# Gate projections as seven block products, with the pre-activations kept in memory

## The chip, the cores and the metric

The kernel runs on one core of one Trainium2 chip. It is one program with one launch. The metric is the time of one execution on the device in microseconds. Three runs of the kernel before took 1441.94, 1443.87 and 1445.47 us; the median is 1443.87 us.

A core has a matrix engine (PE, with its weight loads listed as PEld), a vector engine (DVE), a scalar engine (ACT), a general engine (POOL) and a queue that starts most of the transfers (SP). They run beside each other and wait for each other by semaphores.

## The reference

One layer of a decoder is applied to 1024 prompt tokens and to 64 sample tokens with the same weights. Cut to what the change touches:

```python
p = rms_norm(x, ln1) @ w_in                 # [a | q | k | v | g_a | g_b]
a, q, k, v, g_a, g_b = split(p)             # g_a, g_b: 1024 columns each
a_mix = pooling(a)                          # 512 columns
attn  = dilated_attention(q, k, v)          # 256 columns
mixed = sigmoid(g_a) * (a_mix @ w_pa) + sigmoid(g_b) * (attn @ w_pb)
h = x + mixed @ w_o
y = h + relu(rms_norm(h, ln2) @ w_up)**2 @ w_down
```

All is float32. The widths are: model 1024, pooling 512, attention output 256, feed-forward 4096. The key and value caches of the sample group are also given back, shifted by 8 positions.

## The kernel before, in words

**Layout.** Activations lie transposed: channels on the 128 partitions, tokens along the free axis. All 1088 tokens (`TOK`) are held together, in an order that puts tokens with the same remainder modulo 4 side by side. Two tiles, `act_t[0]` and `act_t[1]`, hold the normalized input as a high and a low part in the narrower float32r form (`split`, lines 113 to 116: ACT writes the high part, DVE subtracts it from the source for the low part). A product of two numbers is made of three passes, high by high, high by low and low by high (`PASSES`). A float32 product of a 128-channel block by a 128-channel block is therefore three PE instructions.

**Weights.** Weights arrive in panels of 256 output columns. `fetch` starts the load of 512 columns into one of three `raw` tiles, and `split` writes the high and low parts into `places`, a tile with room for three panels. `panel` does so at once; `line_up` and `feed` do it ahead of need, paced by PE. `behind_pe` adds a wait of an instruction on a given matrix product, by default the last one that had been issued when the line ran.

**Order.** PE's order is the order of the program text. On the other engines a planner orders the instructions ahead of time, and each engine and each queue then runs its own list in order.

**Stages.** First the pooling input, then q, k and v for the three head groups with the attention blocks between them. Attention's blocks are generators: `step` moves every active one by a yield, and the gate products call it twice per unit, so that the last attention blocks run among the first gate products.

**The gates and the branches** (lines 1163 to 1268). `gate` computes one unit: 128 output channels by a chunk of 384 or 320 tokens, 24 PE instructions, then DVE multiplies by the inverse norms `rb_g` (line 1176) and ACT applies the sigmoid (line 1178). Panels `ga0`, `ga1` and the start of `gb0` run while attention ends. When it has ended, `branches` reads pooling and attention results back (`raw_b`) and splits them into `ab`. Then a loop over d = 0 to 3 takes 256 output channels at a time: six units of g_a, six of g_b, and for each unit `pa_` (four channel blocks of w_pa, 12 instructions) and `pb_` (6 instructions with w_pb). DVE multiplies and adds; the result is split. Since `act` is still being read by later gates, the first six of the eight 128-channel blocks of the result are stored to memory (`mix_d`) and come back over POOL's queue (line 1267) at the end; the last two are written directly.

**After that**, w_o runs by token halves of 544 tokens as two times 272 columns (`ph`), and the feed-forward layer forms both its products from seven block products: `products` computes 24 instructions of 128x272 (line 1477), `put` splits a quarter of weights (lines 1403 and 1404), and `run` works a queue of (prepare weights, products, post) with preparation three entries ahead and loads a given number of entries ahead. The copies of the shifted caches (line 1794) are spread over the whole run by waiting on chosen weight splits.

## Time and profile before

| What | Value |
|---|---|
| Median of three runs | 1443.87 us |
| Profiled execution | 1445.38 us |
| Its span, first to last instruction | 1443.6 us |
| PE busy | 1428.8 us (99%) |
| PE weight loads busy | 1376.5 us (95%) |
| DVE busy | 884.7 us (61%) |
| ACT busy | 718.2 us (50%) |
| POOL busy | 230.6 us (16%) |
| Mean granted PE clock | 0.996 |
| Moved by transfers | 279.04 MB, mean 193 GB/s |

The page of the profile starts with the busy time of each engine and its share of the span. It then shows the chain of work that ended last, followed back from the last instruction, as shares by engine and line; the same chain can be listed in order of time. Groups of instructions are listed by line, engine, operation and tile as "out<-in", with the busy time of the group, the mean duration of one in ns, and after the second bar the idle time of the engine just before them with what ended it. A window row gives, for a stretch of time, its length, and the busy time of each engine with the number of instructions in brackets, then the granted PE clock, the share of the transfer engines and the rate moved.

### The profile page before, as it was taken

Reading aid. Unit: us, or ns where it says so; the run is one execution under the profiler, and the core shown is the slowest. Engines: PE = TensorE matmul, PEld = TensorE weight load, DVE = VectorE, ACT = ScalarE, POOL = GpSimd, SP = SyncE. Lnnn points to the kernel's source line nnn. Section 1 sums busy time; section 2 is a strip of 40 time slices with the busy share of each in tenths; the row PEclk is TensorE's granted clock in tenths of the full one; section 3 lists DMA queues with packets and bytes.
Section 4 is the critical chain, followed back from the end, with each engine's and each line's share of the span. In section 5 each row is a group of like instructions: output and inputs, shape, how many; then the busy total and the mean of one; then the engine's idle time right before and its main releaser. Section 6 shows DMA issues by size and latency. Waiting matters only on the chain.

```text
span 1443.6 us, 28367 instructions
## 1 busy us (share of the span) xinstructions
PE 1428.8 (99%) x10765; PEld 1376.5 (95%) x10765; DVE 884.7 (61%) x1685; ACT 718.2 (50%) x1904; POOL 230.6 (16%) x297
## 2 busy tenths in 40 slices
PE   9999999999999999999999999999999999999998
PEld 8988877878899999999999999999999999999998
DVE  7665575766764552425567877656665586664566
ACT  9566755778634222214435545545444444444453
POOL 1711355555500100000000000000000000000100
PEclk9999999999999999999999999999999999999999
DMA  6311788744555654539656667566567987677574
GB/s 212 111 48 61 215 195 219 199 113 99 148 148 161 208 193 156 183 85 284 210 177 219 225 221 247 184 212 225 186 196 243 320 281 252 219 228 228 183 265 173
DMA packets 169303, 279.04 MB, mean 193 GB/s; under 512 B 33735, under 2 KB 88333, under 8 KB 167118
## 3 DMA queue, kind: packets, MB, share of 16 engines
q1 hardware_dynamic: 161390, 226.89, 50.3%
q0 software_dynamic: 7776, 50.34, 11.0%
q8 instruction: 84, 1.38, 0.4%
q14 instruction: 53, 0.43, 0.1%
HBM read 216.56 MB, written 104.26 MB: 222 GB/s over the span
## 4 chain that ended last, share of the span: by engine, by line
PE 94%; DVE 2%; ACT 1%; DMA 1%; issue 1%; POOL 1%; SPq 0%; DVEq 0%; POOLq 0%; ACTq 0%
PE pd L1755 23%; PE pz L1477 22%; PE ph L184 7%; PE pga L184 7%; PE pgb L184 7%; PE pqk L184 6%; PE pv L184 4%; PE pa L184 3%; PE a L306 3%; PE pb L184 2%; PE pq L184 1%; PE pk L184 1%; DMA raw_qkv<-in_w_in_dram 1%; PE sg0b L637 1%; PE pog0b L667 1%
## 5 line engine op out<-in xcount | busy, mean ns | idle before, releaser
L1755 PE MATMUL pd<-places 128*128 128x272 f32 x2688 | 334.7, 287 | 0.0
L1755 PEld LDWEIGHTS pd<-places 128*128 128x128 f32 x2688 | 334.6, 188 | 0.0
L1403 ACT ACTIVATE places<-raw_d 128x544 fp32r<-128x544 f32 (+1 forms) x176 | 110.8, 646 | 159.9 <-DMA raw_d<-z_d 63.1
L1404 DVE TENSOR_TENSOR places<-raw_d,places 128x544 fp32r<-128x544 f32 (+1 forms) x176 | 122.4, 711 | 94.2 <-ACT places L1403 92.8
L1794 POOL DMA_DIRECT2D out_kv_sample_dram<-in_cache_kv_dram x96 | 47.0, 492 | 830.8 <-ACT places L1403 531.3
L1477 PE MATMUL pz<-act,places 128*128 128x272 f32 x912 | 119.2, 289 | 0.0
L1477 PEld LDWEIGHTS pz<-act,places 128*128 128x128 f32 x912 | 116.5, 188 | 0.0
L184 PE MATMUL pga<-act,places 128*128 128x384 f32 (+1 forms) x576 | 100.5, 333 | 0.0
L184 PE MATMUL pgb<-act,places 128*128 128x384 f32 (+1 forms) x576 | 97.9, 327 | 0.0
L184 PEld LDWEIGHTS pga<-act,places 128*128 128x128 f32 x576 | 96.7, 191 | 0.8 <-issue 0.6
L184 PE MATMUL ph<-act,places 128*128 128x272 f32 x768 | 97.3, 289 | 0.0
L184 PEld LDWEIGHTS ph<-act,places 128*128 128x128 f32 x768 | 96.5, 188 | 0.3 <-ACT places L114 0.2
L184 PEld LDWEIGHTS pgb<-act,places 128*128 128x128 f32 x576 | 95.4, 188 | 0.0
L1477 PE MATMUL pz<-act,apart 128*128 128x272 f32 x624 | 82.0, 289 | 0.0
L1477 PEld LDWEIGHTS pz<-act,apart 128*128 128x128 f32 x624 | 79.9, 188 | 0.1
L600 POOL TENSOR_TENSOR mr<-ms,mhalf 128x4 f32<-128x4 f32 (+2 forms) x39 | 52.3, 1342 | 105.1 <-DVE ms L599 105.0
L184 PE MATMUL pqk<-places,act 128*128 128x512 f32 x240 | 61.0, 403 | 1.1 <-ACT qk L605 1.1
L1477 PE MATMUL pz<-places 128*128 128x272 f32 x432 | 56.4, 287 | 0.0
L184 PEld LDWEIGHTS pqk<-places,act 128*128 128x128 f32 x240 | 44.6, 192 | 11.2 <-ACT qk L605 1.3
L1477 PEld LDWEIGHTS pz<-places 128*128 128x128 f32 x432 | 55.0, 188 | 0.0
L805 POOL TENSOR_TENSOR pck<-pck,qs 128x256 f32<-128x256 f32 x64 | 47.9, 780 | 44.0 <-DMA pck<-in_cache_kv_dram 25.5
L184 PE MATMUL pa<-ab,places 128*128 128x384 f32 (+1 forms) x288 | 51.4, 326 | 0.0
(390 smaller groups left out, 2623.7 us busy)
## 6 DMA issues: line engine op xcount, KB each, us to landing
out_kv_sample_dram<-in_cache_kv_dram POOLq DMA_DIRECT2D x72, 480.0 KB, 5.4
raw_d<-z_d SPq DMA_DIRECT2D x112, 272.0 KB
z_d<-t SPq DMA_DIRECT2D x84, 272.0 KB
raw_d<-in_w_down_dram SPq DMA_DIRECT2D x80, 256.0 KB
raw_u<-in_w_up_dram SPq DMA_DIRECT2D x64, 256.0 KB
raw_qkv<-in_w_in_dram SPq DMA_DIRECT2D x36, 256.0 KB
pck<-in_cache_kv_dram SPq DMA_DIRECT2D x32, 256.0 KB
pcv<-in_cache_kv_dram SPq DMA_DIRECT2D x32, 256.0 KB
```

Source lines behind the costliest of these rows:

```text
L184: last_mm[0] = t_.matmul(out, lhs(a, k), rhs(b, k), start=(j == 0), stop=(j == len(terms) - 1))
L306: last_mm[0] = t_.matmul(pts[m][:, :n], wt[:, a, kk, m * P:(m + 1) * P], act4[b][kk][:, :, part4(c)], start=(p == 0 and kk == 0), stop=(p ...
L600: g_.tensor_tensor(r[:n, :H], ms[:n, :H], mhalf[:n, :H], op=ALU.pow)
L637: t_.matmul(sc[e][:, hp, j * P:(j + 1) * P], qT[rows, hp, :], kT[rows, 2 + hp, :], start=True, stop=True)
L667: t_.matmul(po[e * HD:(e + 1) * HD, hp, :], vr[:, h * HD:(h + 1) * HD], pTs[e][:, hp * nk + j, :], start=(j == 0), stop=(j == nk - 1))
L805: behind_pe(g_.tensor_tensor(t[:, n], t[:, n], qs[:, :256], op=ALU.mult))
L1403: ins = s_.activation(view(t[:, 0]), src, AF.Copy)
L1404: v_.tensor_tensor(view(t[:, 1]), src, view(t[:, 0]).bitcast(F32), op=ALU.subtract)
L1477: last_mm[0] = t_.matmul(x[:, c, :Q], A[:, a, k * P:(k + 1) * P], Bv(b, k, c), start=(first and n == 0), stop=(n == len(terms) - 1), skip_ ...
L1755: last_mm[0] = t_.matmul(chain[t][:, c, :Q], A[:, a, t * P:(t + 1) * P], Z[:, b, c * Q:(c + 1) * Q], start=(fresh and f == 0 and n == 0), ...
L1794: ins = g_.dma_start(d, a)
```

## The change

Both gate projections take the form that the feed-forward layer already has. Each panel of 256 gate columns is a product of a 2 by 2 block matrix of weights (output halves m, input halves a) with a 2 by 2 block matrix of the input (input halves, token halves j of 544 tokens). It is formed from seven block products instead of eight, using sums of weight blocks and sums of input blocks.

- In the early phase, while attention ends, the two products "11" and "21" of each of the eight panels run (16 products of 24 instructions, two banks each). They use the first token half. The first is written to memory (`pg_d`), the accumulated pair is one quarter of the result (`g_d`). `step` is called after each half product and once more after the product.
- `make_sums(k)`, called after products 3, 5, 7 and 9, reads the rows of x for one channel block of each input half (tile `gx`, one buffer), scales them by ln1 and the inverse norms, and forms the sums T1, T3, T2, the block "22" and T4. T1 and "22" overwrite the second token half in `act`; T2 and T3 go to `places`; T4 goes through memory (`t4_d`).
- `finish_attention` closes the attention pools and changes the PSUM layout; it is tried after every fourth product.
- The other five products of each panel (`gate_group`) go through the queue of `enqueue` and `run`, with `load_gate` bringing the panel. The results are pre-activations and are stored to `g_d`.
- The second linear products with w_pa and w_pb run by token halves: all four weight panels stay in `places` (`put_ab`), `ab_part` reads back pooling and attention results, `ab_unit` reads two rows of `g_d`, applies the sigmoids, multiplies, adds and splits straight into `act`. `mix_d` is no longer used.
- The cache copies wait on the weight splits of the gate stage (`marks_g`) instead of `throttle`. Several helpers (`right`, `products`, `put`, `run`) move up in the text; `step` of the feed-forward queue is renamed `enqueue`, and `later` there `lazy`.

```diff
+    def make_sums(k):
+        v = [gx.tile([P, H], F32, name=f"gv{n}_{k}", tag=f"gv{n}") for n in range(4)]
+        for a in range(2):
+            x = gx.tile([P, TOK], F32, name=f"gx{a}_{k}", tag="gx")
+            kk = 4 * a + k
+            dma(x, i["xT"][:, kk, :])
+            for j in range(2):
+                v_.scalar_tensor_tensor(two(v[2 * a + j]), by_token(x, j), ln1[:, kk:kk + 1], two(rb_g[:, half(j)]),
+                                        op0=ALU.mult, op1=ALU.mult)
+        v11, v12, v21, v22 = v
+        def sum_to(n, out, a, b):
+            v_.tensor_tensor(out, a, b, op=ALU.subtract)
+            split(*(t[:, k, :] for t in T[n]), out)
+        sum_to(1, v11, v12, v11)
+        sum_to(3, v12, v22, v12)
+        sum_to(2, v11, v22, v11)
+        split(*(t[:, k, :] for t in T["22"]), v22)
+        v_.tensor_tensor(v21, v21, v11, op=ALU.subtract)
+        dma_st(t4_d[k], v21)
...
+    for n, (f, a) in enumerate(order):
+        fetch_first(n + 5)
+        if a == 0:
+            open_x[f] = bank_pair(f"pg{f}")
+        products(open_x[f], ready.pop(n), B["21" if a else "11"], a == 0, between=step)
+        ready[n + 3] = put_first(n + 3)
+        t = row_tile(1 + a, f)
+        for c in range(2):
+            v_.tensor_tensor(two(t)[:, c], open_x[f][c][:, :Q], rb_g[:, c * Q:(c + 1) * Q], op=ALU.mult)
+        dma_st(g_d[f, 0][:, half(0)] if a else pg_d[f], t)
+        if n in (3, 5, 7, 9):
+            make_sums((n - 3) // 2)
+        step()
+        if n % 4 == 3 and psx is None and not active and not waiting:
+            finish_attention()
...
+    for k in range(4):
+        t = row_tile(2, f"t4_{k}")
+        dma(t, t4_d[k])
+        split(T[4][0][:, k, :], T[4][1][:, k, :], t)
...
+    def load_gate(f):
+        raws[f] = [rr(gq, [P, 1024], F32, name=f"rawg{f}_{a}", tag="rawg", bufs=4) for a in range(2)]
+        for n in range(0, 2048, 512):
+            behind_pe(dma(raws[f][n // 1024][:, n % 1024:n % 1024 + 512], gate_panel(f)[:, n:n + 512]))
...
+        loads.setdefault(max(0, len(queue) - 4), []).append(get_back)
+        enqueue(lambda: summed(1, quarter(f, 1, 0), quarter(f, 1, 1), ALU.add),
+                lambda A: products(fresh(5), A, B["T1"], True), post5, lambda: load_gate(f), 7)
+        enqueue(lambda: summed(2, by_tile(sums[1]), quarter(f, 0, 0), ALU.subtract),
+                lambda A: products(fresh(6), A, B["T2"], True), post6)
+        enqueue(lambda: summed(3, quarter(f, 0, 0), quarter(f, 1, 0), ALU.subtract),
+                lambda A: products(fresh(7), A, B["T3"], True), post7)
+        enqueue(lambda: summed(4, quarter(f, 0, 1), by_tile(sums[2]), ALU.subtract),
+                lambda A: products(more(q["x5"]), A, B["22"], False), post3)
+        enqueue(lambda: put_gate(quarter(f, 1, 1), True),
+                lambda A: products(more(q["x7"]), A, B["T4"], False), post4)
...
+        def load():
+            for x in range(2):
+                g[x] = rr(gab, [P, H], F32, name=f"gg{x}_{j}{d}{m}", tag=f"gg{x}", bufs=4)
+                behind_pe(dma(g[x], g_d[4 * x + d, m][:, half(j)]))
...
+        def post():
+            for x in range(2):
+                s_.activation(g[x], g[x], AF.Sigmoid)
+                v_.tensor_tensor(two(g[x]), two(g[x]), xs_of(g["x"][x]), op=ALU.mult)
+            v_.tensor_tensor(g[0], g[0], g[1], op=ALU.add)
...
-    late = [t for t in throttle[13:-8] for _ in range(8)]
+    late = list(marks_g)
```

More of the change, by code (lines that the diff above doesn't have):

```diff
@@ L1210, in early @@
-    def early(x, d, wt, n):
-        ts = []
-        for c, m in units[n]:
-            ts.append(gate(x, d, c, m, wt, 12 if x == "a" else 3))
-            if ab is None and not active and not waiting:
-                branches()
-        return ts
-    abp = psc = None
-    sga0 = early("a", 0, wga, slice(0, 2))
-    wga1 = by_k(panel(i["w_in"][12], "ga1", after=marks[1:2] * 4))
-    sga0 += early("a", 0, wga, slice(2, 5))
-    wgb = by_k(panel(i["w_in"][15], "gb0", after=marks[4:5] * 4))
-    sga0 += early("a", 0, wga, slice(5, 6))
@@ L1295, in decoder_step @@
+    prep, mm, post = queue.pop()
+    queue.append((prep, mm, lambda: (post(), turn_to_ab())))
+    at = len(queue)
+    for j in range(2):
+        for d in range(4):
+            for m in range(2):
+                ab_unit(j, d, m)
+    for k in range(6):
+        loads.setdefault(at + 1 + k, []).append(lambda k=k: lazy.append(lambda: ab_part(1, k)))
+    run()
+    gabs.close()
+    abs_.close()
+    rows_s.close()
     wq = pool("wq", reuse_waits="tile")
@@ L1470, in make_versions @@
             B[f"T{n}"] = version(*sums_at[n])
[L1472 to L1486 removed]
+    sums, firsts, rest = {}, {}, []
     def then(f):
@@ L1628, in post @@
                 store_z(f, 6, t4)
[L1629 removed]
+            enqueue(lambda: weights(1, 1), lambda A: products(banks(q["x7"]), A, B["T4"], False), post)
         return p1, p5, p2, p6, p7, p3, p4
@@ L1705, in rows_half @@
             for t in range(4):
-                later.append(lambda t=t: (new_row(t), s_.copy(by_token(rows[t], 0), two(hs[t][:, half(0)]))))
+                lazy.append(lambda t=t: (new_row(t), s_.copy(by_token(rows[t], 0), two(hs[t][:, half(0)]))))
     ZI = {2: 1, 4: 6, 1: 0, 5: 3, 6: 4, 7: 5, 3: 2}
```

377 lines of the change are left out of this document (226 added, 151 removed).

## The prediction, made before the changed kernel ran

> **What bounds the kernel now.** I read the page first: busy times, then the shares of the chain that ended last. PE is busy for 1428.8 of 1443.6 us and holds 94% of the chain. Work taken from PE therefore shortens the run, unless a wait replaces it.
>
> ```profile
> PE 1428.8 (99%) x10765; PEld 1376.5 (95%) x10765; DVE 884.7 (61%) x1685; ACT 718.2 (50%) x1904; POOL 230.6 (16%) x297
> ...
> PE 94%; DVE 2%; ACT 1%; DMA 1%; issue 1%; POOL 1%; SPq 0%; DVEq 0%; POOLq 0%; ACTq 0%
> ```
>
> Next comes the chain of waits in order of time, for the rates of the products that are changed. The columns are start, length, engine, group and number of instructions.
>
> ```profile
> 534.56 24.00 PE pga L184 x144
> 558.56 8.32 PE pgb L184 x48
> 566.88 2.09 PE pa L184 x12
> 568.97 1.04 PE pb L184 x6
> ...
> 584.58 3.52 PE pgb L184 x24
> ...
> 597.39 1.76 PE pa L184 x12
> 600.03 24.00 PE pga L184 x144
> ...
> 806.82 297.48 PE pz L1477 x2368
> ```
>
> A unit of 24 gate products takes 8.32/2 = 4.16 us with 384 columns and 3.52 us with 320. A b panel (four and two units) is 23.68 us; an a panel is the 24.00 us row. The 128x272 products of the first feed-forward layer run at 297.48/2368 = 125.6 ns. These two pairs of numbers price most of the change.
>
> The third view is windows of time. It shows what covers PE in the gate stage, which lasts from the first gate product at 384.67 us to the first product of w_o at 665.34 us.
>
> ```profile
> core 0: us, PE busy (x) PEld busy (x) DVE busy (x) ACT busy (x) POOL busy (x), PEclk, DMA share, GB/s
> 384.67:433.85 49.18, 46.13 (x321) 43.53 (x320) 30.61 (x83) 17.41 (x50) 7.18 (x9) 0.93 0.49 143
> 384.67:665.34 280.67, 277.62 (x1725) 275.02 (x1724) 131.57 (x269) 81.35 (x171) 25.19 (x42) 0.99 0.51 162
> 391.00:397.00 6.00, 5.82 (x26) 5.60 (x27) 2.93 (x12) 2.69 (x10) 0.00 (x0) 0.50 0.44 137
> 764.00:807.00 43.00, 42.73 (x336) 42.13 (x335) 39.28 (x48) 29.22 (x43) 3.54 (x5) 1.00 0.80 257
> 807.00:1104.00 297.00, 297.00 (x2367) 297.00 (x2368) 196.12 (x302) 145.03 (x240) 14.15 (x29) 1.00 0.63 209
> ```
>
> Over the whole gate stage DVE has 131.57 us of work in 280.67 us. The stage starts differently: until 433.85 us the last attention blocks still run among the gate products, DVE is already at 30.61 of 49.18 us, and PE idles 49.18 - 46.13 = 3.05 us. The timeline shows those idles.
>
> ```profile
> 388.64 0.49 PE L637 MATMUL sg0b<-qkTg0b,qkTg0b 64*128 64x128 f32 x2 [0.95 <-DVE qkTg0b L623]
> ...
> 391.18 0.58 PE L637 MATMUL sg0b<-qkTg0b,qkTg0b 64*128 64x128 f32 x1 [2.06 <-ACT pTg0b L659]
> ```
>
> **The change part by part.** *Gate products.* Eight panels, each 2 output halves by 2 token halves by 2 input halves, become seven block products instead of eight. Before: 4 x 24.00 + 4 x 23.68 = 190.7 us. After: 8 panels x 7 products x 24 instructions x 125.6 ns = 168.8 us, so 21.9 us less. Of this, 16 products (48.2 us) form the early phase, and 40 (120.6 us) come afterwards from the queue, five per panel.
>
> The Trainium skill, page TensorE: Matmul & The Clock Gate (section "Wait — 56ns, not 53.3ns?") gives N/2.4 GHz plus 2.5 ns per instruction, which for 272 columns is an estimate of 115.8 ns; the 1344 gate instructions would then take 155.7 us. The 125.6 ns row disagrees, and the row is used.
>
> *Second linear products (w_pa, w_pb).* Before: per panel 4 x (2.09 + 1.04) + 2 x 2.64 (from 597.39 to 600.03 us) = 17.8 us, 71.2 us in all. After: 16 units x 36 instructions x 125.6 ns = 72.3 us. That adds 1.1 us.
>
> *Attention's tail.* Its PE work stays. The stage's first 15 half units are counted by this row (180 instructions), and one of them ran at half speed after the idle:
>
> ```profile
> 384.67:433.85 49.18, 34.59 (x180) 31.27 (x181) 3.76 (x7) 0.93 0.49 143
> ```
>
> ```profile
> 393.25 4.14 PE pga L184 x12
> ```
>
> Eleven halves at 2.08 us and four at 1.76 us are 29.9 us; the slow one adds 2.06 us; so attention itself holds 46.13 - 29.9 - 2.06 = 14.2 us of PE. Attention now advances three steps per 3.01 us product, two of them back to back, where it had two per 4.16 us. Its softmax and copies get less cover. Extra PE idle lies between -3 us (the 3.05 us of now vanish) and +10 us (each of the three remaining blocks meets the present 3.05 us again); I take +4, nearest to one repetition of the row. Without extra idle, PE ends the early phase at 384.67 + 48.2 + 14.2 + 3.05 + 2.06 = 452.2 us; with it, at 456.2.
>
> *The sums.* `make_sums`, four calls, is new DVE and ACT work in just this phase. Costs by the vector engine's groups:
>
> ```profile
> L1368 DVE TENSOR_TENSOR y<-ph,xr 128x544 f32<-128x544 f32 x8 | 9.0, 1124 | 3.0 <-DMA xr<-in_xT_dram 2.8 <-PE ph L184 0.2
> ...
> L1371 DVE TENSOR_TENSOR y<-ph,y 128x544 f32<-128x544 f32 x8 | 5.8, 722 | 8.7 <-PE ph L184 8.7
> ```
>
> ```profile
> L115 DVE TENSOR_TENSOR places<-raw_ga,places 128x512 fp32r<-128x512 f32 x6 | 4.8, 823 | 0.4 <-ACT places L114 0.4
> ...
> L1176 DVE TENSOR_TENSOR sga<-pga,rb_g 128x384 f32<-128x384 f32 x5 | 2.8, 558 | 11.4 <-PE pga L184 11.4
> ...
> L115 DVE TENSOR_TENSOR places<-raw_gb,places 128x512 fp32r<-128x512 f32 x4 | 2.7, 686 | 1.7 <-ACT places L114 1.7
> ...
> L1176 DVE TENSOR_TENSOR sga<-pga,rb_g 128x320 f32<-128x320 f32 x2 | 1.0, 486 | 0.1
> ```
>
> A call has 4 scaled reads of x with a token stride of four elements. L1368 reads x the same way and takes 1124 ns where L1371 takes 722. Then 4 subtractions and 4 low parts at those 722 ns: 10.3 us per call, 41.1 us in all. Writing the 16 products out through `rb_g` is 32 operations of 272 columns; 558 ns at 384 and 486 at 320 give 0.43 us, 13.8 us in all. The 12 weight quarters of `put_first` cost 0.69 us each (the `raw_gb` row), 8.3, and about three of the first four quarters remain, 2.1. Attention's own part is 30.61 - 4.8 - 2.8 - 2.7 - 1.0 = 19.3 us. The first queued product (`post5`'s group 0) needs T1 in full but not the six last operations of the fourth call (4.3 us), and one addition of its own weights (0.69). Together 81.0 us, with one ACT split behind it:
>
> ```profile
> L1403 ACT ACTIVATE places<-sm 128x512 fp32r<-128x512 f32 x36 | 22.6, 628 | 24.7 <-PE pz L1477 21.5 <-DVE t L1597 2.4 <-DVE sm L1571 0.8
> ```
>
> So by DVE the first queued product starts at 384.67 + 81.0 + 0.63 = 466.3 us; I take 466. That assumes DVE has no idle time. Against it stands the window from 764 to 807 us, where the same kind of sums are formed for the feed-forward layer: DVE busy 39.28 of 43 us, 91%, PE 42.73. At 91% the start would be 384.67 + 89 + 0.63 = 474. On the other side, DVE's durations overlap their successors' in the timeline, so the sum is also an upper count. Both ends go into the range.
>
> *The first queued panel.* `load_gate(0)` is issued behind the last early product (`behind_pe`), and both its halves, four DMAs of 256 KB, must land before the first sum of weights. Nothing else is queued on PE there. Each DMA takes 0.42 us to issue, and 2.53 to 5.55 us to land:
>
> ```profile
> L1514 SPq DMA_DIRECT2D raw_u<-in_w_up_dram x64: 332/424/2743, 784.5 to 1064.0; - x64
> ```
>
> ```profile
> 162.65 5.55 DMA raw_qkv<-in_w_in_dram
> ...
> 274.00 2.53 DMA raw_qkv<-in_w_in_dram
> ```
>
> Issue 1.7, landing about 3, addition 0.69, split 0.63: 6.0 us, so PE stands from 452.2 until at least 458.2 us. With 456.2 it is 462. DVE's 466 is later and decides. `get_back`, `load_gate(1)` and the stores of the last rows wait with that load on SP's queue; `put_gate` waits on ACT and DVE. The T4 reload is needed 12 us later only.
>
> *The clock.* From 391 to 397 us, after 3 us idle out of 4, the granted clock is 0.50 with PE busy 5.82 us, a loss of 2.9 us; the single slow half unit lost 2.06. After a stand of ten microseconds I add 2.5. The Trainium skill, TensorE: Matmul & The Clock Gate (section "Part 1: The HAM clock gate"), says that one idle window of 3.4 us halves the clock until 3.4 us of sustained work have passed. That rule speaks against the change, and by it the loss would be an estimated 1.7 us; the trace agrees on the half, but held it nearly 6 us.
>
> *Queued groups.* A group of five needs 9 DVE operations on weights (0.69) and 5 on 544 columns (0.72): 9.8 us in 15.1 us, 65%. The feed-forward stage runs 196.12 in 297.00 us, 66%, with PE busy throughout. So this stage costs only its products.
>
> *Products with w_pa, w_pb.* Per unit DVE has four operations of 0.72, ACT two sigmoids and a split of about 0.65; a unit lasts 4.52 us. In the first token half `ab_part(1, k)` (4.3 us) and `put_ab` (8.3 us) are added: 35.6 us of DVE in 36.2 us of PE. I take no stall, with bounds 0 and +5 us. The loads of `ab_unit` at the switch arrive within the first unit's products, which need only resident tiles.
>
> *Moved transfers.* On POOL's queue the six returns of `mix_d` (L1267) go; on SP's queue 18 stores of `mix_d` and 14 loads of `raw_b` go, and about 165 issues replace 76 in all: at 0.42 us that is 69 us of the stage. They move about 47 MB by their sizes, with 26 cache copies of about 0.48 MB more: 59 MB in 276 us, or 215 GB/s, against 162 now. The feed-forward stage carries 209 GB/s with PE never idle. I cost this at nothing; its cover is the leads of four to seven products. The cache copies are paced by `marks_g` instead of `throttle`, 64 marks of 238 against 80 of 254, so about four move out of this stage.
>
> *Sum.* 466.3 + 2.5 + 120.6 + 72.3 = 661.7 us for the first product of w_o, 665.34 before: 3.6 us less. After that nothing changes but names; the first panel of w_o finds its place free two units ahead. As terms: -21.9 + 1.1, and 17.2 us of the gain returned by early phase, stand and clock. The profiled execution took 1445.38 us with a span of 1443.6; 1445.4 - 3.6 = 1441.8. The median of the runs is 1.5 us below that execution, so the forecast is 1440.3.
>
> **The rivals.** *Only the load is paid.* If DVE interleaves the sums so well that T1 is ready first, and attention's tail gets no new idle, PE starts at 458.2: 661.7 - 8.1 = 653.6, time 1432.1. For it speaks that PE lost only 0.27 us of the 43 us in the similar stretch; against it, that DVE there had no attention to serve.
>
> *Slower: the sums run in series.* `make_sums` has one x buffer, and each call needs two x rows of 544 KB one after the other. If the sums stay behind the fourth product in DVE's in-order queue (384.67 + 12.1 of products + 5.1 of idle and slow clock + about 11 of attention = 413 us), then 41.1 us, 12 products' output and weights at 1.55 us (18.6), and four exposed halves of a load (10) end at 483, or 480 without the last six operations. Then w_o starts 13.7 us later than in my sum: 1454. It decides from the point where the first queued product starts after 470 us. For it speaks the 91% above and DVE waiting in order behind a DMA; against it, that operations are free to be listed earlier, as `raw_gb`'s low parts were among attention's.
>
> *DVE bounds the w_pa stage.* 35.6 in 36.2 us leaves no room; with 91% it takes 39, and PE, two units ahead at most, loses 3 to 5 us: 1445. Against it: some of `put_ab` is done during the last group.
>
> That seven products do not take less PE time than eight would need 272-column products at 190.7/1344 = 142 ns; 2368 of them ran at 125.6, so I give it nothing.
>
> **How the numbers follow.** A measurement of this kernel tells about 0.2% (2.9 us) from no change. The likeliest case, DVE setting the restart at about 466 us, has 0.42; its own range, restart between 461 and 471, is 1435 to 1445. Load only: 0.25. Sums in series: 0.23. DVE-bound w_pa stage: 0.10. Of the likeliest, 0.28 lies over 0.2% faster, 0.11 within, 0.03 slower; the load case is faster, the serial case slower, the last 0.08 within and 0.02 slower. So faster 0.53, same 0.19, slower 0.28. The range reaches from the load case to the serial case, 1431 to 1455.
>
> **What would show it.** Gate products at about 125.6 ns each, 1344 of them, right; near 142 ns, wrong. One idle stretch on PE of about 10 us around 455 to 466 us, released by DVE's sums (my case), by the `rawg` DMA (load only), or after 475 us with x's DMA ahead of DVE (series). A clock near 0.5 for some 5 us behind it. Busy DVE above 90% from 400 to 465 us. No PE idle from there to w_o; idle in the w_pa units would be the third rival. Wrong altogether I would be if the queued groups waited on SP's loads all along, since that stage has been costed at its products alone.

## The result: 1464.8 us, slower by 1.4%, and where the profile shows it

The changed kernel took 1464.81 us (median of five runs, 1461.69 to 1467.47) beside 1445.47 us for the kernel before on the same chip. The ratio is 1.0138, with a 95% interval of 1.0118 to 1.0159. The profiled execution took 1463.3 us, with a span of 1461.5 us against 1443.6 before.

The page of the changed kernel opens with the busy times:

```profile
PE 1415.0 (97%) x11101; PEld 1360.9 (93%) x11101; DVE 969.8 (66%) x1783; ACT 743.9 (51%) x1930; POOL 226.0 (15%) x291
```

PE lost 13.8 us of busy time (1428.8 to 1415.0), as the change promised in kind, and yet the span grew by 17.9 us. PE's idle time rose from 14.8 to 46.5 us, by 31.7. The windows show in which stage. They are the early phase (first gate product to the end of the last early product), the whole stage up to w_o, the queue of 40 products, and the products with w_pa and w_pb:

```profile
core 0: us, PE busy (x) PEld busy (x) DVE busy (x) ACT busy (x) POOL busy (x), PEclk, DMA share, GB/s
384.71:469.98 85.27, 69.48 (x525) 65.90 (x523) 76.61 (x156) 28.44 (x68) 7.78 (x10) 0.90 0.72 208
384.71:680.27 295.56, 264.38 (x2061) 260.36 (x2060) 216.25 (x371) 113.80 (x204) 18.00 (x31) 0.95 0.73 227
482.64:604.90 122.26, 122.26 (x961) 122.26 (x962) 78.90 (x122) 36.79 (x61) 8.75 (x18) 0.98 0.74 233
604.90:680.27 75.37, 72.63 (x577) 72.20 (x577) 52.73 (x81) 44.73 (x70) 0.97 (x2) 1.00 0.71 233
```

In the early phase PE was busy for 69.48 of 85.27 us and idle for 15.8, while DVE was busy for 90% of it. Between 469.98 and 482.64 us PE stood altogether. The queue of 40 products then ran without a gap. w_o starts at 680.27 us, 14.9 us later than before (665.34), and the rest of the run is 3.0 us longer (1461.5 - 680.27 = 781.2 against 778.3).

PE's waits between 384 and 700 us, with the total, the number and the longest:

```profile
PE pg L1226 <- ACT places L1233: 12.7, 1, 12.7
PE pg L1226 <- DVE g L1335: 5.1, 4, 2.6
PE sft L1048 <- DVE sres L1043: 4.3, 1, 4.3
PE pab L1492 <- DVE gg L1498: 2.7, 2, 1.5
PE twg0u L739 <- DVE hl L714: 2.6, 1, 2.6
PE sg0b L650 <- DVE qkTg0b L636: 2.2, 1, 2.2
PE sg0b L650 <- ACT pTg0b L672: 1.5, 1, 1.5
```

All but the first and the last end with DVE. Two of these, `sft` and `twg0u`, are small matrix products of attention; the DVE operations `sres` and `hl` they wait for are small ones of attention, and stood among the sums in DVE's list. Some rows of that list, with steps of the sums (`gv`) right ahead of `sres`:

```profile
416.36 0.75 DVE L115 TENSOR_TENSOR act<-gv,act 128x544 fp32r<-128x544 f32 x1
...
418.19 0.75 DVE L1296 TENSOR_TENSOR gv<-gv,gv 128x544 f32<-128x544 f32 x1
418.82 0.32 DVE L1043 COPY sres<-osm 128x256 f32<-128x256 f32 x1
```

The `g` waits are the early products' results that DVE had not yet written out of PSUM, the memory that the products are written to, so that PE had no free bank of it. PE's waits in order of time:

```profile
407.18 0.38 PE L739 MATMUL twg0u<-cst,hl 128*24 128x128 f32 x2 [2.63 <-DVE hl L714]
419.29 1.09 PE L1048 MATMUL sft<-cst,sres 128*128 128x64 f32 x4 [4.31 <-DVE sres L1043]
449.89 3.25 PE L1226 MATMUL pg<-act,places 128*128 128x272 f32 x24 [2.64 <-DVE g L1335]
482.64 5.02 PE L1226 MATMUL pg<-act,places 128*128 128x272 f32 x24 [12.66 <-ACT places L1233]
```

The last row is the first queued product. It waits for ACT's split of its weights, and that for the load of the panel, which had been held behind the last early product. SP's queue at that place, and two DVE operations:

```profile
470.57 0.38 SPq L1370 DMA_DIRECT2D rawg<-in_w_in_dram  x1
473.60 0.32 SPq L1356 DMA_DIRECT2D g_t<-t_d  x1
474.01 0.38 SPq L1297 DMA_DIRECT2D t_d<-gv  x1
474.44 0.95 SPq L1370 DMA_DIRECT2D rawg<-in_w_in_dram  x2
...
475.97 1.45 SPq L1370 DMA_DIRECT2D rawg<-in_w_in_dram  x3
```

```profile
465.51 0.73 DVE L115 TENSOR_TENSOR act<-gv,act 128x544 fp32r<-128x544 f32 x1
...
481.23 0.69 DVE L1392 TENSOR_TENSOR sm_g<-rawg,rawg 128x512 f32<-128x512 f32 x1 [1.08 <-DMA rawg<-in_w_in_dram]
```

The first of eight `rawg` transfers went out with PE's end; the next ones stood behind a reload of T4 (`g_t`), which waited 2.6 us for the store of an early product's row (`g_d<-g`) to land, and a store of T4. T1's last low part, the first of the two DVE rows, was done at 466.24 us, before PE had ended its early phase. The sum of weights that the first queued product needs began at 481.23, fifteen microseconds later. So DVE's sums did not release the first queued product; the panel's load did, and it began only when PE's delayed early phase had ended.

### The profile page after: what moved, and what is told of

Read it like the earlier page. It is cut to its first block, busy times and chain, and to the rows that moved or that the text cites. A ratio compares the mean times of both kernels' runs of the same rounds, so it can differ in the third digit from the quotient of the medians.

```text
span 1461.5 us, 29372 instructions
## 1 busy us (share of the span) xinstructions
PE 1415.0 (97%) x11101; PEld 1360.9 (93%) x11101; DVE 969.8 (66%) x1783; ACT 743.9 (51%) x1930; POOL 226.0 (15%) x291
## 5 line engine op out<-in xcount | busy, mean ns | idle before, releaser
L1226 PE MATMUL pg<-act,places 128*128 128x272 f32 x576 | 82.0, 303 | 17.8 <-ACT places L1233 12.7
L1226 PEld LDWEIGHTS pg<-act,places 128*128 128x128 f32 x576 | 78.6, 201 | 19.4 <-ACT places L1233 17.1
L1492 PE MATMUL pab<-ab,places 128*128 128x272 f32 x384 | 50.7, 288 | 2.7 <-DVE gg L1498 2.7
L319 PE MATMUL a<-act,places 128*128 128x384 f32 (+1 forms) x288 | 50.2, 332 | 1.8 <-ACT act L297 1.2
L1492 PEld LDWEIGHTS pab<-ab,places 128*128 128x128 f32 x384 | 48.9, 188 | 3.2 <-DVE gg L1498 3.2
```

The source lines that it names most:

```text
L319: last_mm[0] = t_.matmul(pts[m][:, :n], wt[:, a, kk, m * P:(m + 1) * P], act4[b][kk][:, :, part4(c)], start=(p == 0 and kk == 0), stop=(p ...
L1226: last_mm[0] = t_.matmul(x[c][:, :Q], A[:, a, k * P:(k + 1) * P], Bv(b, k, c), start=(first and n == 0), stop=(n == len(terms) - 1), skip_ ...
L1492: last_mm[0] = t_.matmul(q[x][:, c, :Q], w.rearrange("p s n -> p (s n)")[:, at:at + P], rhs, start=(n == 0), stop=(n == len(terms) - 1))
```

## The experiments

Medians are given, with the ratio to the kernel before on the same chip and its 95% interval; the runs come from several chips, so kernels are best compared by these ratios. "w_o" is the time at which the first product of w_o starts in the profiled execution (665.34 before, 680.27 after).

**Without the sums.** The first question was how much of the loss is the sums and how much the load.

```diff
-        if n in (3, 5, 7, 9):
-            make_sums((n - 3) // 2)
...
-        dma(t, t4_d[k])
+        dma(t, pg_d[k])
```

> make_sums is left out with its loads, so T1 to T4 hold other data and the result of the gates is not the reference's; all matrix products stay. Rival D: the waits of the early products for the writing out of rows (5.1 us) vanish, attention's waits fall to the 3 us of the kernel before, the early phase shrinks from 85 us to about 74, and the stand before the queued products to the bare load of 6 us: time 16 to 20 us less, 1445 to 1449. Theory L and S together: the stand stays at 9 us or more and attention's waits stay above 8 us; time 5 to 8 us less.

1448.97 us, ratio 1.0025 (1.0012 to 1.0037); w_o at 666.9. The early phase as a window (it begins 1.5 us ahead of this run's first gate product, at 386.20 us), PE's two largest waits, SP's queue at the restart, and the window from the first issue of the load to the sum of weights for the first queued product:

```profile
384.70:456.44 71.74, 65.83 (x537) 63.62 (x536) 44.22 (x114) 21.18 (x58) 9.03 (x12) 0.95 0.64 179
```

```profile
PE pg L1226 <- ACT places L1233: 12.0, 1, 12.0
PE sg0b L650 <- DVE qkTg0b L636: 4.4, 2, 2.3
```

```profile
459.16 0.32 SPq L1354 DMA_DIRECT2D g_t<-pg_d  x1
459.53 0.42 SPq L1368 DMA_DIRECT2D rawg<-in_w_in_dram  x1
460.48 2.44 SPq L1368 DMA_DIRECT2D rawg<-in_w_in_dram  x5
```

```profile
459.53:467.05 7.52, 0.00 (x0) 0.00 (x0) 2.11 (x3) 1.28 (x2) 0.49 (x1) 0.50 0.88 270
```

PE's early phase ended at 456.44 us, where the prediction had 456.2; with the sums it ended at 469.98. The waits of `sft`, `twg0u` and for `g` are gone. So the sums moved the end of the early phase by 13.5 us, and its length by 15.0 (85.27 to 70.24 us, from the first gate product on). This edit takes the sums' loads and ACT's splits away together with DVE's operations, so it prices the sums as a whole and not DVE's part of them. The load alone still kept PE standing for 12.0 us, though DVE was busy for only 2.1 of the 7.5 us in the last window: its first issue came 3.1 us after PE's end, behind a reload of T4 in the same queue, and eight transfers of two panels were under way together (270 GB/s for 7.5 us, 2.0 MB), where the prediction had the landing time of a lone transfer.

**The first two panels loaded early, alone and without the sums.** Their loads are not held behind a matrix product.

```diff
-            behind_pe(dma(raws[f][n // 1024][:, n % 1024:n % 1024 + 512], gate_panel(f)[:, n:n + 512]))
+            ins = dma(raws[f][n // 1024][:, n % 1024:n % 1024 + 512], gate_panel(f)[:, n:n + 512])
+            if f > 1:
+                behind_pe(ins)
```

> The loads of the first two queued panels no longer wait behind the last early product; nothing else changes. Theory L (the stand of 12.66 us before the first queued product is the late load): the stand shrinks to what the sums leave, T1 being written at about 472 us with PE free at 470, so 3 to 5 us remain, the clock stays full, and the time falls by 8 to 11 us to about 1455. Rival D (the vector engine's sums set the restart, as the prediction had it): the stand stays above 9 us and the time moves by less than 3 us.

1466.35 us, ratio 1.0144 (1.0129 to 1.0159); w_o at 681.1: no gain. The 12.7 us stand is gone, and the time comes back in pieces. The largest of them stands at the second queued product:

```profile
482.80 1.27 PE L1226 MATMUL pg<-places 128*128 128x272 f32 x4 [5.74 <-ACT places L114]
```

`places` by L114 is T2. The preparation of the queued weights now took DVE's time before the sums were complete, and DVE waited 3.6 us in one place for a row of x, whose load was issued among the panel's and took 7.9 us until it was used, for 3.8 in the changed kernel. So the sums were late instead of the load: T1 was done at 474.2 us, for 466.24 in the changed kernel (not the 472 from which the expectation started).

> No make_sums and the first two queued panels loaded early (the gates' result is not the reference's). In the run without sums PE stood 12.0 us before the first queued product although the vector engine had almost nothing to do. Theory P (two covers, vector work and panel load, each long enough alone): the stand falls to 2 us or less and the slow clock behind it goes, 11 to 14 us less than without sums alone, 1435 to 1438, faster than the kernel before. If the stand has another cause (the reload of T4 ahead on ACT and SP), it stays above 6 us and the time above 1443.

1443.48 us, ratio 0.9992 (0.9978 to 1.0006); w_o at 661.0. With the sums gone the same edit was worth about 5 us. So the load and the sums hide each other: taking away the load alone gave nothing, the sums alone 16 us, both 21 us. And with both gone the kernel was only as fast as before.

**T4 brought back later.** The reload of T4 (which needs the last sums) stood ahead of the panel on SP and in ACT's list; here it is listed at the second queue entry, with the panel early.

```diff
-    for k in range(4):
-        t = row_tile(2, f"t4_{k}")
...
+    loads.setdefault(1, []).insert(0, load_t4)
```

> As the run with the early panels, and the reload of T4 is listed behind the first queued product's preparation instead of ahead of it, since the SP queue stood 2.6 us for it in the trace and ACT 4.6 us. Theory L: 2 to 4 us less than with the early panels alone, the restart then following T1 directly. If the sums alone decide, no difference from that run beyond 2 us.

1464.97 us, ratio 1.0138 (1.0110 to 1.0165), w_o at 683.7. Nothing gained: the waits for T2 are as in the run before, 5.6 and 1.3 us, and so are those for `g`, 6.8 us.

**Attention's pace.** The third `step()` per early product is dropped, with and without the sums, and without the sums with the early panel.

```diff
         if n in (3, 5, 7, 9):
             make_sums((n - 3) // 2)
-        step()
```

> The third call of step per early product is left out, so attention advances once per half product of 1.5 us instead of three times per 3.0 us. Theory S (the denser steps give attention's chain too little cover): the waits of sft (4.3 us), twg0u (2.6) and sg0b (3.7) shrink together by 5 us or more, the slow clock between 408 and 426 us goes, time 6 to 10 us less. Rival D (the sums on the vector engine delay attention's small operations): the waits fall by less than 3 us, time within 3 us of the changed kernel.

1476.85 us, ratio 1.0226 (1.0199 to 1.0253), w_o at 694.7. The waits grew:

```profile
428.87 1.08 PE L1048 MATMUL sft<-cst,sres 128*128 128x64 f32 x4 [8.34 <-DVE sres L1043]
444.86 0.59 PE L739 MATMUL twg0u<-cst,hl 128*24 128x128 f32 x2 [6.21 <-DVE hl L714]
```

> No make_sums, and attention advanced by two steps per early product instead of three. With the sums in place two steps cost 12 us. Theory Q (fewer steps only hurt because attention's small vector operations then stand behind more of the sums): without sums the two settings differ by less than 3 us, 1446 to 1452. Rival (a longer tail of attention costs by itself): again 8 us or more slower than without sums alone, above 1457.

1448.59 us, ratio 1.0032 (1.0018 to 1.0045): the same as without the sums and with three steps. The pace itself is free. It matters only beside the sums; that a longer attention has more of its small operations standing among them is my reading of the two larger waits, and no run took it apart.

> No sums (the gates' result is not the reference's), early panels, two steps per product: what the seven products would bring if their sums were free. The run without sums and with two steps reached w_o at 662.2 us with a stand of 12.1 us in it. Theory: w_o is reached at 649 to 653 us, 12 to 16 us ahead of the kernel before, time 1433 to 1438. If the restart without the stand still loses to other waits, as it did with three steps (660.9 us): 1441 or more.

1443.76 us, ratio 0.9990 (0.9979 to 1.0001), w_o at 659.3. The first product with T4 waited here, and a half clock followed (0.52 and 0.50 in the windows from 471 to 474 and from 474 to 478 us):

```profile
471.30 1.02 PE L1226 MATMUL pg<-gt,places 128*128 128x272 f32 x3 [3.38 <-DVE gt L1411]
```

**Four row tiles for T4, without the sums.** T4's four rows come back through two tiles, so that two of the reloads wait for the splits of the first two. The DVE operation in the row above (L1411) is not a split of T4. It reads the bank that this product adds to, and it stood in DVE's list behind splits of T4 that waited for the reloads. Here T4 has four tiles; the rest is as in the run before, with the early panel and two steps.

```diff
-        return rr(rows_p, [P, H], F32, name=f"g{n}_{name}", tag=f"g{n}", bufs=2)
+        return rr(rows_p, [P, H], F32, name=f"g{n}_{name}", tag=f"g{n}", bufs=4 if n == 2 else 2)
```

> Left out: the sums of the input (T1, T2, T3 and 22 hold whatever lies there, T4 is read from another tensor), so the gates are not the reference's. The kernel without sums, with the panel loaded early and two steps, took 1443.8 us although its PE reached the end of the early phase at 448.4 us; the first product with T4 waited 4.1 us in pieces (3.4, 0.5 and 0.2), because the four rows of T4 come back through two row tiles. Here there are four row tiles. If that reload is what eats the rest of the gain, the wait goes with its half clock, w_o starts at about 654 instead of 659.4 us and the time is 1438 to 1440. If the queue that issues the reload is the limit, nothing changes: 1443.8.

1441.64 us, ratio 0.9968 (0.9951 to 0.9985), w_o at 654.75, the earliest of all runs. The row of the same product is now

```profile
469.77 0.65 PE L1226 MATMUL pg<-gt,places 128*128 128x272 f32 x3 [1.36 <-DVE gt L1411]
```

The wait shrank to 2.5 us in three pieces rather than vanishing. With input sums that cost nothing, 0.3% is the most that any run showed of the change. The profiled execution was the fastest of six (1438.12 us). Its span was 7.3 us shorter than that of before, though w_o started 10.6 us earlier; 3.3 us were lost after w_o.

**Relief for DVE.** Four ways of moving work from DVE, or its waits. First the strided reads of x to ACT and the subtractions to POOL, alone and with the early panel and late T4.

```diff
-                v_.scalar_tensor_tensor(two(v[2 * a + j]), by_token(x, j), ln1[:, kk:kk + 1], two(rb_g[:, half(j)]),
-                                        op0=ALU.mult, op1=ALU.mult)
+                s_.activation(two(v[2 * a + j]), by_token(x, j), AF.Copy, scale=ln1[:, kk:kk + 1])
+                v_.tensor_tensor(v[2 * a + j], v[2 * a + j], rb_g[:, half(j)], op=ALU.mult)
...
-            v_.tensor_tensor(out, a, b, op=ALU.subtract)
+            g_.tensor_tensor(out, a, b, op=ALU.subtract)
```

> The strided, scaled reads of x go to ACT (16 copies of about 1.18 us), DVE multiplies contiguous rows (0.72 instead of 1.13 us), and the 16 subtractions go to POOL, which is idle there. DVE loses 18 us of the 41 us of the sums. Theory D (vector work delays attention and the rows): PE's early phase ends 5 to 8 us sooner, time 1456 to 1460, the stand for the panel staying near 12 us. If POOL slows DVE's operations as much as it relieves them: within 3 us of the changed kernel.

1471.51 us, ratio 1.0188 (1.0171 to 1.0205): slower than the change. Groups of the early phase, of this kernel:

```profile
L115 DVE TENSOR_TENSOR act<-gv,act 128x544 fp32r<-128x544 f32 x8 | 10.0, 1250 | 3.0 <-ACT act L114 2.9
L115 DVE TENSOR_TENSOR places<-gv,places 128x544 fp32r<-128x544 f32 x8 | 8.3, 1038 | 0.1
L1289 POOL TENSOR_TENSOR gv<-gv,gv 128x544 f32<-128x544 f32 x12 | 18.3, 1536 | 55.6 <-DVE gv L1285 46.0 <-DVE ce L707 9.7
```

and of the changed kernel:

```profile
L1289 DVE TENSOR_TENSOR gv<-gv,gv 128x544 f32<-128x544 f32 x12 | 8.3, 726 | 0.0
L115 DVE TENSOR_TENSOR act<-gv,act 128x544 fp32r<-128x544 f32 x8 | 5.8, 724 | 0.7 <-ACT act L114 0.7
L115 DVE TENSOR_TENSOR places<-gv,places 128x544 fp32r<-128x544 f32 x8 | 5.8, 730 | 0.6 <-PE pg L1226 0.6
```

A subtraction took 1.54 us on POOL for 0.73 on DVE, and the low parts on DVE 1.04 and 1.25 us in the mean for 0.72 to 0.73, so part of what was taken from DVE came back as longer operations on it. The means mix two kinds: the low parts of `act` that began at 419.93, 438.62, 456.91 and 472.26 us, while POOL subtracted, took 1.35 to 1.99 us, and those at 409.71, 429.83, 449.46 and 467.33 us, while it did not, took 0.72 or 0.73. The Trainium skill, SBUF — State Buffer (section "Who interferes with whom"), says that a DVE instruction with two SBUF inputs and a GpSimd instruction that reads SBUF share one port pair, so that one of them waits; the lengthened low parts, which have two SBUF inputs, agree with that. DVE also waited 9.1 us for ACT's reads; what of the loss is due to which, this run does not separate.

> The relief of the vector engine together with early panels and the later reload of T4. Theory P: both covers are taken away at once, so the gain is more than the sum of the two alone (0 and about 6 us): 12 to 18 us less than the changed kernel, 1447 to 1453. Rival: the vector engine still decides the restart and no more than the relief's own gain shows, 1456 to 1460.

1464.67 us, ratio 1.0142 (1.0109 to 1.0175), w_o at 677.1. Beside the early panel the same relief ends level with the change.

Next, three buffers for x (the serial case of the prediction rested on the single one), the reads on ACT without POOL, and all of it with the early panel and the late T4:

```diff
-            x = gx.tile([P, TOK], F32, name=f"gx{a}_{k}", tag="gx")
+            x = gx.tile([P, TOK], F32, name=f"gx{a}_{k}", tag=f"gx{(2 * k + a) % 3}")
```

> Three x buffers instead of one in make_sums, all else as in the changed kernel. This tests the prediction's rival of the sums in series, whose price was four exposed loads of 2.5 us. If x's loads serialize the sums: the vector engine's idle time in the early phase (about 9 of 85 us) falls and the restart comes 5 to 10 us sooner, 1455 to 1460. If the vector engine's own work and order decide: less than 3 us, since in the trace it waited only 1.0 us for x.

1464.38 us, ratio 1.0135 (1.0118 to 1.0152), w_o at 681.0: as the change. The loads of x were not what held DVE.

> The strided, scaled reads of x on ACT, the multiplication by the norms on DVE, the subtractions staying on DVE: POOL stays out. In the relief with POOL, DVE's low parts took 1.04 to 1.25 us instead of 0.73 and the time rose by 6 us. If that slowing was the whole cause: DVE now loses 7.5 us of work (16 times 1.19 to 0.72), the early phase ends 4 to 7 us sooner, 1457 to 1461. If the longer chain of a sum (ACT, then DVE) is the cause: 1466 to 1472, with DVE waiting 8 us or more for ACT's reads.

1467.27 us, ratio 1.0155 (1.0138 to 1.0173), w_o at 684.3: not faster, though DVE has 7.5 us less to do. It waited 6.5 us for ACT's reads instead, near the 7.5 that it was relieved of.

> Three x buffers, reads on ACT, early panels, the later reload of T4, together. If vector work and the panel load cover each other and both are relieved: restart near 470 us, no slow clock behind it, 1450 to 1456. If the preparation of the queued products only takes the vector engine's place from the sums again, as with early panels alone: 1460 or more.

1463.77 us, ratio 1.0132 (1.0117 to 1.0148), w_o at 684.7. The restart stand was gone; attention waited 7.4 us in one place, and the first product with T4 6.8 us in two pieces. The second of them, 4.4 us, was for ACT's split of a row of T4, which had itself waited 3.7 us for the reload.

**Place or amount.** Whether the sums hurt by where they stand or by how much they are. First the sums two products later, with the early panel, the late T4, two x tiles and four row tiles; then the same with the reads on ACT.

```diff
-        if n in (3, 5, 7, 9):
-            make_sums((n - 3) // 2)
+        if n in (5, 7, 9, 11):
+            make_sums((n - 5) // 2)
```

> All of the computation. The sums are called after products 5, 7, 9 and 11 instead of 3, 5, 7 and 9, with the panel loaded early, T4 brought back one entry later, two x tiles and four row tiles. Theory amount (DVE has more work than the early phase is long): DVE's demand is the same, so only the waits of the attention tail (7 to 9 us) go and a wait for T1, T2 or T3 of the same size comes; w_o starts at 675 to 684 us, time 1457 to 1465. Theory place (the sums stand in DVE's list ahead of attention's small operations): the early phase ends near 458 us, w_o starts near 662, time 1444 to 1448.

1466.22 us, ratio 1.0139 (1.0122 to 1.0156), w_o at 680.6. The planner put the sums among attention's operations all the same: the first read of x ran at 404.0 us, for 402.4 in the changed kernel, and the last at 470.4 for 468.1. PE's largest wait for attention doubled. Three rows of DVE's list, with a step of a sum (`gv`) ahead of attention's `cw` and `sres`, and the row of PE:

```profile
424.87 1.18 DVE L1284 SCALAR_TENSOR_TENSOR gv<-gx,cols,rb_g 128x544 f32<-128x544 f32 x1
425.96 0.18 DVE L709 TENSOR_TENSOR cw<-ce,md 128x24 f32<-128x24 f32 x1
...
427.08 0.30 DVE L1043 COPY sres<-osm 128x256 f32<-128x256 f32 x1
```

```profile
427.52 1.08 PE L1048 MATMUL sft<-cst,sres 128*128 128x64 f32 x4 [9.95 <-DVE cm L711]
```

So calling them later hardly moved them and did not protect attention, and this run does not test a list in which attention goes first.

> All of the computation. As the run with later sums, and the strided reads of x on ACT, which leaves DVE 16 multiplications of 0.72 us in place of 16 operations of 1.19 us, 7.5 us less. Theory amount: 5 to 8 us below the run with later sums. Theory place: 1444 to 1448 as that one. A third, that ACT's list then holds up the evacuations and the splits: not below that run.

1461.26 us, ratio 1.0107 (1.0082 to 1.0132), w_o at 677.1: 5.0 us below the run with later sums, at the low end of the 5 to 8 us that 7.5 us less of DVE's work should give. The two intervals overlap, and the same move had gained nothing with the sums at their old place, so this shows little of DVE's amount.

Last, the 16 strided reads taken away whole, 19 us of DVE's work, with the sums at their old place. The four `gv` tiles are also two deep here, which the cut does not show:

```diff
-            dma(x, i["xT"][:, kk, :])
-            for j in range(2):
-                v_.scalar_tensor_tensor(two(v[2 * a + j]), by_token(x, j), ln1[:, kk:kk + 1], two(rb_g[:, half(j)]),
-                                        op0=ALU.mult, op1=ALU.mult)
+            for j in range(2):
+                dma(v[2 * a + j], i["xT"][:, kk, half(j)])
```

> Left out: the scaling of x by ln1 and the inverse norms in the sums (rows of x are loaded straight into the four tiles and subtracted unscaled), so the gates are not the reference's. DVE has 16 operations of 1.19 us, 19.1 us, less in the early phase; panel loaded early, T4 one entry later, four row tiles, sums after products 3, 5, 7 and 9. Measured ends: 1465.0 with all 41 us of sums (same early panel), 1443.5 with none. Theory amount, in proportion: 1465 - 21.5 * 19.1/41.1 = 1455. If only what exceeds the phase counts (81 us of demand less 19.1 fits into 71.7 us): 1444 to 1447. Theory place: the waits of attention stay, 1460 or more.

1461.3 us, ratio 1.0111 (1.0096 to 1.0127), w_o at 676.8. Only 3.7 us below the run with the early panel and late T4 (the intervals overlap), and not the 10 us of proportion. DVE had finished the sums at 447 us, but attention's waits stayed (4.2 us at `sft`, 2.9 at `twg0u`), as the theory of place had it. Then PE waited for what came behind transfers. One row of SP's queue, two of ACT, one of PE:

```profile
448.51 6.30 SPq L1369 DMA_DIRECT2D rawg<-in_w_in_dram  x6
```

```profile
463.02 0.63 ACT L1233 ACTIVATE places<-raw_gf 128x512 fp32r<-128x512 f32 x1 [8.47 <-DMA raw_gf<-in_w_in_dram]
...
488.78 0.66 ACT L114 ACTIVATE ab<-g_ab 128x544 fp32r<-128x544 f32 x1 [3.69 <-DMA g_ab<-amix_d]
```

```profile
490.88 5.80 PE L1226 MATMUL pg<-gt,places 128*128 128x272 f32 x24 [5.12 <-DVE gt L1413]
```

The weights of the last early products (`raw_gf`) were now queued behind the early panel's loads, and ACT waited 8.5 us for them. The wait of 5.1 us at the first product with T4 was not for T4, whose splits were done by 485.3 us. It was for DVE's addition L1413, which reads the bank that this product adds to. That stood in DVE's list behind the split of a pooling row (`ab`), for whose load ACT had waited 3.7 us. So with less work on DVE, the transfers around the restart and the order of DVE's list take over, and the price does not follow DVE's amount alone. How much of the 13.5 us is amount and how much is order in DVE's list stays open; that they are the sums' is shown by the run without them.

No version tried with the whole computation beat the kernel before.

## Why the prediction was wrong, point by point

**The work taken from PE: right.** The queued gate products, in a stretch after the restart (x896 in 112 us, 125.0 ns each), ran at the 125.6 ns of the feed-forward row or slightly under it:

```profile
492.00:604.00 112.00, 112.00 (x896) 112.00 (x895) 70.02 (x109) 30.98 (x51) 7.78 (x16) 1.00 0.73 227
```

The queue of 40 took 122.26 us, where 120.6 and 2.5 for the clock had been summed. PE's busy time fell by 13.8 us and not by the 21.9 - 1.1 = 20.8 of the products; the other 7 us went to half clocks, as shown below.

**The step that failed: two paths taken as a maximum.** The prediction let PE end its early phase at 456.2 us, added the load (462), set DVE's 466 beside it and took the later. DVE's own path came out, with T1 done at 466.24 us. The other path failed, since the prediction had given it no part of DVE's new work. PE's early phase was not beside DVE's work but ran through it: attention's products wait for DVE's small operations, and the early products for DVE to write them out. So its end moved by 13.8 us, to 469.98 (456.44 without the sums), and the load came behind that. In the changed kernel the terms stand in series: 469.98 + 12.66 = 482.64. The working had counted attention's 19.3 us and the write-outs' 13.8 us in DVE's demand, but not asked who waits for them.

**The tail's extra idle: mis-sized.** Taken as +4 us between -3 and +10; the early phase idled 15.8 us, 12.7 more than the 3.05 of before and so outside the bounds. Without the sums it idled 70.24 - 64.33 = 5.9 us, where 3.05 + 4 had been taken. The bounds were drawn from repetitions of the present wait, that is, from a phase in which DVE did not have the sums. Of the 13.8 us by which the end moved, 8.7 are this idle time (15.8 for 7.05) and 5.0 half clocks (below).

**The panel's load: 12.0 us for 6.0.** Even with DVE nearly idle. Left out were the 3.1 us in which SP's queue stood at a reload of T4 that waited for the store of an early product's row to land. From the first issue to the sum of weights it then took 7.5 us, where 1.7 and 3 had been taken; that eight transfers land together is the likely reason, but no run took it apart.

**DVE's demand: its end right, in part by luck.** T1's last low part ended at 466.24 us, where 465.7 had been summed without idle time and about 474 was the upper value. Two misses cancelled. Up to there DVE was busy for 73.6 of 81.5 us, so it idled for 7.9; and it had done 7.4 us less than the 81.0 summed, since two of the reads of x and four write-outs, among others, came only behind T1. Its two new operations over the whole phase:

```profile
L1284 DVE SCALAR_TENSOR_TENSOR gv<-gx,cols,rb_g 128x544 f32<-128x544 f32 x16 | 18.6, 1194 | 1.0 <-DMA gx<-in_xT_dram 1.0
L1335 DVE TENSOR_TENSOR g<-pg,rb_g 128x272 f32<-128x272 f32 x32 | 13.4, 440 | 3.1 <-PE pg L1226 2.2 <-DMA rb_g<-r_d 0.8
```

1194 ns for 1124 taken, 440 for 430. A DVE busy for more than 90% from 400 to 465 us, one of the signs named, was seen (59.2 of 65 us).

**The clock: 2.5 us taken, 2.0 measured.** The first queued product took 5.02 us for the 3.01 of a product at full clock. The windows from 474 us on:

```profile
474.00:486.00 12.00, 3.36 (x15) 3.37 (x16) 7.24 (x12) 4.36 (x7) 0.97 (x2) 0.50 1.00 351
486.00:492.00 6.00, 6.00 (x48) 6.00 (x48) 5.61 (x10) 3.64 (x6) 0.49 (x1) 0.96 0.58 177
```

The granted clock was 0.50 up to 486 us and 0.96 in the six microseconds behind it, so the half clock ended about four microseconds after the restart. The Trainium skill, TensorE: Matmul & The Clock Gate (section "Part 1: The HAM clock gate"), gives about 3.4 us of sustained work before the full clock; here the estimate of 1.7 us lost that was worked out from it was nearer than the row of before. What had not been counted are the half clocks inside the early phase: PE's busy time there was 69.5 us for 62.4 of work at full clock (48.2 of products and 14.2 of attention), 7.1 us lost and not 2.06.

**The w_pa stage: within its bounds.** 75.37 us for 72.3, with 2.7 us of waits for `gg`, between the 0 taken and the +5 allowed. The largest of these waits was 0.8 to 3.2 us in the other runs too, so it is a cost of the change by itself.

**After w_o: "nothing changes but names" failed by 3.0 us.** The feed-forward's first stage took about 2.5 us more, part of it in waits at its start, where PE had lost 0.27 us of 43 before; the largest:

```profile
819.03 2.29 PE L1226 MATMUL pz<-act,apart 128*128 128x272 f32 x16 [0.73 <-DVE apart L1234]
```

In the kernels of the experiments the time from the start of w_o to the end was 778.4 to 782.7 us, for 778.3 before. The cache copies fall differently there, but no run tells whether they are the cause; it stays open.

**The rivals.** "Sums in series" gave a restart at 480 us and 1454; the restart came at 482.64. So its direction and the threshold of 470 us were right, but its mechanism, the single x buffer and exposed loads of x, was not: three buffers changed nothing, and DVE waited 1.0 us in all for x. "Load only" was wrong in its price and its cover, though its sign, a restart released by the `rawg` load, is the one that was seen. "DVE bounds the w_pa stage" held in a small way. The sum of the deviations: early phase +13.8 (469.98 for 456.2), stand +2.6 (12.66 where 10.1 had been left between 456.2 and 466.3), queue -0.8, w_pa stage +3.1, after w_o +3.0: 21.7 us from rounded terms, beside the 21.5 between the forecast span (1443.6 - 3.6 = 1440.0) and 1461.5 us. The forecast median of 1440.3 was missed by 24.5 us; the other 3.0 come from the profiled executions, 1.5 us above the median of three runs before and 1.5 us below the median after.

## What to carry to other kernels

When work is added to a secondary engine, do not compare its total with the length of the phase and take the later: list which of the bound engine's own waits end on that engine, since here these waits grew though DVE was idle for a tenth of the phase. Price a load that starts after a stand with all the transfers that start with it, and with what stands ahead of it in its queue. Where two delays end close together, take both away in one experiment before calling either harmless, for removing one alone can show nothing, as it did for the load here.

## What the runs showed of the hardware that was not expected

A POOL subtraction of 128x544 took 1536 ns beside DVE, and DVE's low parts 1250 and 1038 ns in the mean instead of 724 and 730: the low parts of `act` that ran beside a POOL subtraction took 1.35 to 1.99 us each, the others 0.72 or 0.73. While the panel was loaded, from 474 to 486 us, the transfer engines' share was 1.00 and they moved 351 GB/s. Whether more transfers at this place would have lengthened the stand was not tried.
